# First feed-forward block of a two-layer kernel: seven block products of 384 columns in place of eight from the sixth feature on, and the residual kept in DRAM

## The chip, the cores and the metric

One Trainium2 chip; the kernel runs on one core. The metric is the device time of one launch in microseconds, the median of several runs. TensorE is called PE here, its weight loads PEld, VectorE DVE, ScalarE ACT, GpSimd POOL and SyncE SP. SP does nothing but issue transfers in this kernel; POOL may do so too.

## What is computed

A block with two layers on a sequence of 512 tokens and a context of 256 tokens, 1024 wide, all in 32-bit floats. Layer 0 mixes with Fourier transforms and a long convolution; layer 1 is attention over sequence and context. Each layer ends in a feed-forward block. Cut to that block, the reference is:

```python
def _conv_ffn(h, w_up, conv_w, conv_b, w_down):      # h: tokens x 1024, D_FF = 2816
    gate, val = jnp.split(h @ w_up, 2, axis=-1)
    return (jax.nn.silu(_dwconv3(gate, conv_w, conv_b)) * val) @ w_down

for i in range(2):
    sh1, sc1, g1, sh2, sc2, g2 = _adaln(c, w_mod[i], b_mod[i])   # silu(c) @ w_mod + b_mod
    ...
    x = x + g2 * _conv_ffn(_modulate(_rms_norm(x, norm2[i]), sh2, sc2), *ffn)
    if i == 0:
        ctx = ctx + cg2 * _conv_ffn(_modulate(_rms_norm(ctx, norm2[i]), csh2, csc2), *ffn)
```

In layer 0 the block therefore works on 768 columns (512 of x, 256 of the context); in layer 1 on 512. `w_up` has two halves, gate and value. The change is in the block of layer 0.

## The kernel before

**Layout.** Activations lie transposed: 128 features on the partitions, tokens along the free axis. 1024 features are 8 tiles (k = 0 to 7), 2816 are 22 tiles. A tile of 128 of the 2816 is called a feature f below, 0 to 21. The residual lives in SBUF in 8 tiles `xr` of 128 x 768.

**Products.** Each 32-bit operand is split into a high part in PE's reduced 32-bit format (`hi`, L247, on ACT) and the rest (`lo`, L252, on DVE: operand minus high part). `mm3` (L273 to L275) issues three matmuls for one product: high x high, high weight x low, low weight x high. So one 128 x 128 weight tile against n columns costs three matmuls of n columns, each with its own weight load.

**First feed-forward block** (`ffn` with `width == TV`, called by `layer0`). For each f, `products(f)` loads two weight tiles `w_up[0, f, 0]` (gate) and `w_up[0, f, 1]` (value) of 128 x 1024 by SP, splits them, and multiplies each by the 8 tiles of the normed activations, in two pieces of 512 (x, tiles `hh`, `hl`) and 256 columns (context, `hhc`, `hlc`): 2 x 8 x 2 x 3 = 96 matmuls. `up(f)` then does the convolution over three neighbouring tokens (`conv3`, L489 on ACT, L492 and L493 on DVE), silu (L1333), the product with the value half (L1335), and splits the result into `ah`, `al`. After 8, 16 and 22 features `res_proj` does the down-projection of that group: for each of the 8 output tiles m it loads and splits a tile of `w_dn`, multiplies it by the group's activations in the pieces 512 and 256, and adds the gated result to `xr[m]` straight out of PSUM (L1284, on DVE). The last group does all of x first and then all of the context, so that the norm of layer 1 starts beside the context's products; `ahook` also loads the first weights of attention.

**Work put in between.** The modulation vectors (`_adaln`) that are not needed yet are computed on DVE by `gemv_dve` (L358: a row product of a 128 x 1024 tile `wmodT` with the silu of the condition, one for x and one for the context where both are needed; L359 adds the bias). `fill(f)` does three of them after each f from 2 on. 56 tiles `wmodT` are left for this block; the first 24 have both conditions, the last 32 one.

**What sets the order.** In `ffn` of layer 0 the tile framework orders the instructions from the program's order. Other parts are written out by hand, token by token, in strings (`FILTER_ORDER`, `MIX_ORDER`, `ORDER`, `UP_ORDER`): inside `manual_schedule` each engine executes its instructions strictly in the written order. Every engine executes in order anyway: an instruction that waits holds up all that stands behind it on the same engine.

**Second feed-forward block** (`up1`, for layer 1). It is there already in the form that the change brings to layer 0, with blocks of 256 columns: from its fifth feature on the 2 x 2 blocks (gate and value, lower and upper four k, left and right half of the columns) are multiplied with seven block products instead of eight (Winograd's form of Strassen's scheme). Sums of weight blocks (`S1` to `S4`, L2170 to L2180) and, once, sums of activation blocks (`T1` to `T4`) are made on DVE; each has to be split again; the results are joined on ACT (`E1` to `E5`, L2228) and DVE (`C1`, `C2`, `V1`, `V2`, L2244 to L2257). Its order is `UP_ORDER`; its residual `xr` stays in SBUF and is added to by L2318 on DVE.

Of the kernel before, what the change touches and what calls it, by code (L numbers as in the profile page):

```python
# [28 lines left out]
GROUPS = ((0, 8), (8, 16), (16, 22))  # L29
# [117 lines left out]


# [12 lines left out]
class Ring:  # L161
# [9 lines left out]
    def put(self, t):  # L171
        self.left[id(t)] -= 1
        if not self.left[id(t)]:
            self.free.append(t)

# [15 lines left out]
class Builder:  # L191
# [159 lines left out]
    def gemv_dve(self, i, jt, conds=(0, 1), raw=None, row=None):  # L351

        nc = self.nc
        raw = raw or self.wraw(self.I["wmodT"][i, jt])
# [934 lines left out]
    def ffn(self, i, x, hh, hl, width, segs, first_segs, late, fill=None, hook=None, rest=None, early=False, there=()):  # L1289
        nc, I = self.nc, self.I  # L1290
        v = nc.vector
        if width == TV:
            self.gap("afit", 320)
            ax = self.pool("actx", bufs=10)
            self.gap("agap", 160)
            a1 = self.pool("act1")
            self.gap("agap2", 32)
            ac = self.pool("actc", bufs=9)
            act = lambda tag, f=1: Two(self.t(ax, [P, 512], F32R, tag), self.t(ac if f % 10 else a1, [P, 256], F32R, tag + "c"))
        else:  # L1300
            ap = self.pool("actx", bufs=10)
            act = lambda tag, f=1: self.t(ap, [P, T], F32R, tag)
        tm = self.pool(f"ftm{i}", bufs=3)
        acts = {}
        keep = []
        cuts = [slice(a, a + m) for a, m in segs]

        def products(f):
            ws = [self.wload(I["w_up"][i, f, q]) for q in range(2)]
            if early and f >= NF - 4:  # L1310

                n = 128 * (NF - GROUPS[2][0])
                keep.append((act("ah"), act("al")))
                raw = self.wraw(I["w_dn2"][i, len(keep) - 1], n)
                for c in cuts:
                    self.hi(keep[-1][0][:, c], raw[:, c])
                    self.lo(keep[-1][1][:, c], raw[:, c], keep[-1][0][:, c])
            pss = [self.mm(), self.mm()]
            if f == 0:
                todo = [(k, q, a, n) for seg in first_segs for k in range(KD) for q in range(2) for a, n in seg]  # L1320
            else:
                todo = [(k, q, a, n) for q in range(2) for a, n in segs for k in range(KD)]
            for k, q, a, n in todo:
                w = slice(128 * k, 128 * k + 128)
                self.mm3(pss[q][:, a : a + n], ws[q][0][:, w], ws[q][1][:, w], hh[k][:, a : a + n], hl[k][:, a : a + n], k == 0, k == KD - 1)
            return pss

        def up(f):
            pss = there[f] if f < len(there) else products(f)
            g = self.t(tm, [P, width], F32, "fg")  # L1330
            n = width
            self.conv3(g, pss[0], self.col(f"fcw{i}0", f), self.col(f"fcw{i}1", f), self.col(f"fcw{i}2", f), self.col(f"fcb{i}", f), segs)
            nc.scalar.activation(g[:, :n], g[:, :n], AF.Silu)  # L1333
            a = g
            v.tensor_tensor(a[:, :n], g[:, :n], pss[1][:, :n], op=ALU.mult)  # L1335
            ah, al = act("ah", f), act("al", f)
            for c in cuts:
                self.hi(ah[:, c], a[:, c])
                self.lo(al[:, c], a[:, c], ah[:, c])
            acts[f] = (ah, al)  # L1340
            if fill:
                fill(f)

        nxt = 0
        for gi, (f0, f1) in enumerate(GROUPS):
            while nxt < min(f1 + 1, NF):
                up(nxt)
                nxt += 1
# [1186 lines left out]
```

## Time and profile before

| | |
|---|---|
| median of 3 runs | 1526.65 us (1525.8 to 1541.0) |
| the profiled execution's own time | 1528.16 us |
| its span, first to last instruction | 1526.4 us |
| PE busy | 1500.2 us, 98% |
| PEld busy | 1305.4 us, 86% |
| DVE busy | 1153.6 us, 76% |
| ACT busy | 659.3 us, 43% |
| POOL busy | 93.6 us, 6% |
| granted PE clock, mean | 0.996 |
| moved from and to HBM | 169.1 MB, 111 GB/s over the span |

The profile is one execution. Rows of groups give a line of the kernel, engine, operation and tiles, the count, the busy time with the mean duration of one in ns, and the idle time of the engine just before them with what ended it. Durations of matmuls include their way through the array and overlap; the distance from one start to the next says what one costs. DVE's instructions overlap by a little less than 0.1 us in the same way. Rows of a window give, for each engine, busy us and the number of instructions in brackets.

### The profile page before, as it was taken

How to read it: one execution, taken by the hardware profiler on the slowest of the kernel's cores; microseconds unless marked ns; L12 is line 12 of the kernel's file. 1: busy time of each engine (PE TensorE's matmuls, PEld its weight loads, DVE VectorE, ACT ScalarE, POOL GpSimd, SP SyncE). 2: the span in 40 equal slices, each digit the busy share in tenths (PEclk: the TensorE clock that was granted, in tenths of full speed). 3: DMA queues.
4: the chain of work that ended last, by engine and by line, in shares of the span. 5: the costliest groups of instructions: out<-in, count | busy, mean ns of one | idle time of the engine just before them, and what ended most of it. 6: DMA issues, size and time to landing. Idle time of an engine off the chain costs nothing.

```text
span 1526.4 us, 24078 instructions
## 1 busy us (share of the span) xinstructions
PE 1500.2 (98%) x9728; PEld 1305.4 (86%) x9728; DVE 1153.6 (76%) x1979; ACT 659.3 (43%) x999; POOL 93.6 (6%) x110
## 2 busy tenths in 40 slices
PE   7999999999999999999999999999999999999999
PEld 5778888889888888888888897766559999999998
DVE  5799978888988346663355377999987899898873
ACT  4362235324323212222123235988964556555551
POOL 0021126000000000000000000111110000000000
PEclk9999999999999999999999999999999999999999
DMA  9426522452545234541344221000015223332322
GB/s 360 137 94 223 173 67 67 156 171 83 166 155 162 71 110 161 169 155 60 104 134 131 87 85 35 11 15 5 11 42 180 63 77 125 112 114 92 120 91 97
DMA packets 54987, 170.61 MB, mean 112 GB/s; under 512 B 6235, under 2 KB 9629, under 8 KB 53853
## 3 DMA queue, kind: packets, MB, share of 16 engines
q1 hardware_dynamic: 54877, 169.08, 33.2%
q8 instruction: 76, 1.25, 0.3%
q14 instruction: 34, 0.28, 0.1%
HBM read 163.29 MB, written 5.77 MB: 111 GB/s over the span
## 4 chain that ended last, share of the span: by engine, by line
PE 89%; DVE 5%; DMA 2%; ACT 1%; issue 1%; POOL 1%; SPq 0%; ACTq 0%; DVEq 0%; POOLq 0%
PE mm L273 16%; PE mm L274 16%; PE mm L275 16%; PE bank L273 7%; PE bank L275 7%; PE bank L274 7%; PE pv L1808 3%; PE s L273 2%; PE pv L1819 1%; PE s L275 1%; PE s L274 1%; PE ms L275 1%; PE ms L273 1%; PE ms L274 1%; DVE junk L358 1%
## 5 line engine op out<-in xcount | busy, mean ns | idle before, releaser
L247 ACT ACTIVATE wh<-wr 128x1024 fp32r<-128x1024 f32 (+2 forms) x170 | 168.4, 992 | 383.4 <-PE mm L274 272.5
L252 DVE TENSOR_TENSOR wl<-wr,wh 128x1024 fp32r<-128x1024 f32 (+2 forms) x170 | 194.9, 1148 | 51.1 <-ACT wh L247 48.7
L273 PE MATMUL mm<-hh,wh 128*128 128x512 f32 x504 | 198.8, 394 | 1.7 <-DVE tm L493 1.1
L274 PE MATMUL mm<-hl,wh 128*128 128x512 f32 x504 | 197.0, 391 | 2.3 <-DVE hl L428 2.3
L275 PE MATMUL mm<-hh,wl 128*128 128x512 f32 x504 | 196.6, 390 | 0.0
L358 DVE SCALAR_TENSOR_TENSOR junk<-wr,sb 128x1024 bf16<-128x1024 f32 x112 | 138.4, 1236 | 57.0 <-DMA wr<-wmodT 56.9
L274 PE MATMUL mm<-hlc,wh 128*128 128x256 f32 (+1 forms) x488 | 135.9, 279 | 0.0
L273 PE MATMUL mm<-hhc,wh 128*128 128x256 f32 (+1 forms) x488 | 135.9, 279 | 0.0
L275 PE MATMUL mm<-hhc,wl 128*128 128x256 f32 (+1 forms) x488 | 135.6, 278 | 0.0
L273 PEld LDWEIGHTS mm<-hh,wh 128*128 128x128 f32 x504 | 94.7, 188 | 22.4 <-issue 5.3
L275 PEld LDWEIGHTS mm<-hh,wl 128*128 128x128 f32 x504 | 94.6, 188 | 20.2
L274 PEld LDWEIGHTS mm<-hl,wh 128*128 128x128 f32 x504 | 94.7, 188 | 19.8 <-DVE hl L428 3.3
L1284 DVE SCALAR_TENSOR_TENSOR xr<-mm,mod,xr 128x512 f32<-128x512 f32 (+1 forms) x64 | 38.0, 615 | 86.1 <-PE mm L275 86.0
L275 PE MATMUL bank<-act,wl 128*128 128x256 f32 x352 | 97.3, 276 | 0.0
L273 PE MATMUL bank<-act,wh 128*128 128x256 f32 x352 | 97.2, 276 | 0.0
L274 PE MATMUL bank<-act,wh 128*128 128x256 f32 x352 | 97.2, 276 | 0.0
L273 PEld LDWEIGHTS mm<-hhc,wh 128*128 128x128 f32 x488 | 91.7, 188 | 3.9
L274 PEld LDWEIGHTS mm<-hlc,wh 128*128 128x128 f32 x488 | 91.6, 188 | 3.9
L275 PEld LDWEIGHTS mm<-hhc,wl 128*128 128x128 f32 x488 | 91.9, 188 | 0.0
L1760 ACT ACTIVATE S<-s,rks 128x512 f32<-128x512 f32 x96 | 63.1, 688 | 12.7 <-PE s L275 6.3
L275 PEld LDWEIGHTS bank<-act,wl 128*128 128x128 f32 x352 | 66.1, 188 | 0.1
L273 PEld LDWEIGHTS bank<-act,wh 128*128 128x128 f32 x352 | 66.1, 188 | 0.0
(604 smaller groups left out, 4136.8 us busy)
## 6 DMA issues: line engine op xcount, KB each, us to landing
wr<-w_up SPq DMA_DIRECT2D x88, 512.0 KB, 3.7
wr<-wmodT SPq DMA_DIRECT2D x80, 512.0 KB, 3.5
wr<-w_dx SPq DMA_DIRECT2D x24, 384.0 KB, 3.1
wm<-wmod0a SPq DMA_DIRECT2D x8, 1024.0 KB, 8.6
wr<-w_in SPq DMA_DIRECT2D x16, 512.0 KB, 4.3
wr<-w_dn SPq DMA_DIRECT2D x16, 512.0 KB, 3.5
wr<-w_out SPq DMA_DIRECT2D x11, 512.0 KB, 3.5
wr<-w_o SPq DMA_DIRECT2D x8, 512.0 KB, 3.5
```

Of the source, the lines that this page charges most:

```text
L247: self.nc.scalar.activation(dst, src, AF.Copy)
L252: (eng or self.nc.vector).tensor_tensor(dst, src, hi.bitcast(F32), op=ALU.subtract)
L273: mmul(out, wh, xh, start=start, stop=False, **kw)
L274: mmul(out, wh, xl, start=False, stop=False, **kw)
L275: mmul(out, wl, xh, start=False, stop=stop, **kw)
L358: nc.vector.scalar_tensor_tensor(junk, raw, 1.0, self.sb[:, j, :], op0=ALU.mult, op1=ALU.mult, accum_out=acc)
L1284: nc.vector.scalar_tensor_tensor(x[m][:, a2:b2], ps[:, a2 + o : b2 + o], mod[:, 8 * sec + m, c : c + 1], x[m][:, a2:b2], op0=ALU.mult, op1 ...
L1760: nc.scalar.activation(c.S[a, j // 3][:, j % 3, :], c.ps[a, j], AF.Copy, scale=c.s.r[:, g : g + 1])
L1808: nc.tensor.matmul(c.P[64 * a : 64 * a + 64, :], V[:, j, o : o + 64], c.S[a, j // 3][:, j % 3, :], start=j == 0, stop=j == 5, tile_positio ...
L1819: nc.tensor.matmul(c.zz[o : o + 32, :], self.ones32, c.S[a, h][:, i, :], start=i == 0, stop=i == 2, tile_position=(0, o))
```

## The change

- **Up-products of layer 0.** Features 0 to 4 stay plain, but the 768 columns are cut 384 + 384 instead of 512 + 256. From f = 5 on, seven block products `P1` to `P7` of 4 k-tiles x 384 columns take the place of eight. For them the weights get sums S1 to S4 (each 128 x 512) and three more splits (`HA`/`DA`, `H1`/`D1`, `H4`/`D4`, with `HG`/`DG`; plain features split gate and value only). The activations get sums T1 to T4 once (128 x 4 x 384 each, in halves), with T3 written over the right half of the lower k-tiles. The PSUM results are copied by ACT (`E1`, `E2`, `E3`, `E5`) and joined by DVE (`C1`, `C2`, `V1`, `V2`) in SBUF tiles `eg`, `ev`, from which the convolution and the product with the value half now read.
- **Groups of the down-projection.** Six groups (0-3, 4-6, 7-9, 10-12, 13-15, 16-21) for three; groups 0 to 4 in pieces of 384 + 384, the last in 256 + 256 and then 256.
- **Residual.** Before the block's sums begin, SP writes the 8 tiles `xr` to a DRAM tile `xq` each. Groups 0 to 4 don't add on DVE: ACT scales the PSUM result by the gate into one of two SBUF slots `st` (`XA`, three instructions), and POOL issues a transfer that adds the slot to `xq[m]` in DRAM (`XD`). Before the last group's adds SP loads `xq` back into new tiles `xr`; the last group adds on DVE as before.
- **Order.** The whole block from its first product on stands in a `manual_schedule` over PE, DVE, ACT, SP and POOL; its middle is a string `UP0_ORDER` of 1066 tokens, its beginning and end are written as code. 48 of the 56 tiles of `gemv_dve` are in the string (`LM` loads, `GV` computes), 8 in the end.
- **PSUM.** Six banks of 512 columns and two `ms` replace three tiles of two banks and two `ms`, for this block alone.

The core of the diff (the removed `ffn`, allocations, and parts that repeat the second block are cut):

```diff
-GROUPS = ((0, 8), (8, 16), (16, 22))
+GROUPS0 = ((0, 4), (4, 7), (7, 10), (10, 13), (13, 16), (16, 22))
+PLAIN0 = 5
+GEMV0 = 48
...
+UP0_ORDER = """
+LV:1 LG:2 LV:2 LM:0 LG:3 EA:0 GB:0 GV:0 LM:1 VB:0 HV:1 EB:0 DV:1 CV:0 LV:3 CX:0 GB:1 HG:2 GV:1 CC:0 LM:2 VA:1 DG:2 HV:2 SI:0 DV:2 LG:4 EA:1 EB:1 MU:0
...
+LW:1.1 DA:7 CV:6 GV:13 P7:6 XA:0.7 XD:0.7 HW:1.1 P1:7 CX:6 E3:6 LM:14 V2:6 CC:6 P2:7 V1:6 SI:6 S1:7 E1:7 MU:6 S3:7 AH:6 DW:1.0 H1:7 AL:6 DN:1.0 LW:1.2
...
+P7:21 HW:5.1 C2:21 CV:21 DW:5.1 CX:21 DN:5.0 HW:5.2 E3:21 DW:5.2 CC:21 V2:21 SI:21 DN:5.1 V1:21 MU:21 AH:21 AL:21 DN:5.2
+"""
...
+    def up0(self, x, H, hh, hl, steps, first, gl):
+        d0 = self.pool("d0", space=bass.MemoryType.DRAM)
+        xd = [self.t(d0, [P, TV], F32, f"xq{m}") for m in range(KD)]
...
+        W2 = TV // 2
+        cols = slice(0, W2), slice(W2, TV)
+        def piece(out, f, q, h, ks=range(KD)):
+            w = wt[f, q]
+            for k in ks:
+                s = slice(128 * k, 128 * k + 128)
+                self.mm3(out[:, 0:W2], w[0][:, s], w[1][:, s], hh[k][:, cols[h]], hl[k][:, cols[h]], k == 0, k == KD - 1)
+        def block(out, w, o, b, start):
+            for k in range(4):
+                s = slice(o + 128 * k, o + 128 * k + 128)
+                self.mm3(out[:, 0:W2], w[0][:, s], w[1][:, s], b[0][:, k, b[2]], b[1][:, k, b[2]], start and k == 0, k == 3, not start)
+        with self.tc.manual_schedule(engines={ENG.PE, ENG.DVE, ENG.Activation, ENG.SP, ENG.Pool}):
+            take, f2, a2 = steps
...
+            for k in range(KD):
+                for q in range(2):
+                    piece(ps[0, q, 0], 0, q, 0, [k])
+                if k == 0:
+                    take(KD)
+                if k == 2:
+                    f2(step=0)
+                if k == 6:
+                    f2(step=1)
+            ps[1, 0, 0] = R["mm"].get(1)
+            piece(ps[1, 0, 0], 1, 0, 0)
+            a2(0, 0)
...
+            for d in (5, 6, 7, 0, 1, 4, 2, 3):
+                nc.sync.dma_start(xd[d], x[d])
+            buffers()
...
+            def T(j, h):
...
+                if j in (1, 3):
+                    v.tensor_tensor(t_, part(plus, 0), part(less, 0), op=ALU.subtract)
+                    v.tensor_tensor(t_, t_, part(plus, 1), op=ALU.add)
+                    v.tensor_tensor(t_, t_, part(less, 1), op=ALU.subtract)
+                else:
+                    v.tensor_tensor(t_, part(plus, 0), u_, op=ALU.subtract)
+                    v.tensor_tensor(t_, t_, part(plus, 1), op=ALU.add)
+            def S1(f):
+                r = raw[f, 1]
+                v.tensor_tensor(r[:, half[1]], r[:, half[0]], r[:, half[1]], op=ALU.add)
+            def P1(f):
+                ps[f, "a"] = R["mm"].get(2)
+                block(ps[f, "a"], wt[f, 0], 0, up["B"][0], True)
+            def E1(f):
+                nc.scalar.copy(up["eg"][:, cols[0]], ps[f, "a"][:, 0:W2])
+            def join(dst, src):
+                v.tensor_tensor(dst, src[:, 0:W2], dst, op=ALU.add)
...
+            def XA(g, m):
+                p = ps.pop(("d", g, m))
+                s = st[g, m] = R["st"].get(1)
+                gate = lambda c: mod[:, 40 + m, c : c + 1]
+                nc.scalar.activation(s[:, 0:W2], p[0][:, 0:W2], AF.Identity, scale=gate(0))
+                nc.scalar.activation(s[:, W2:CX], p[1][:, 0 : CX - W2], AF.Identity, scale=gate(0))
+                nc.scalar.activation(s[:, CX:TV], p[1][:, CX - W2 : W2], AF.Identity, scale=gate(1))
+            def XD(g, m):
+                nc.gpsimd.dma_start(xd[m], st[g, m], accum_op=ALU.add)
+                R["st"].put(st.pop((g, m)))
+            def LM(i):
+                load(("m", i), I["wmodT"][gl[i][0], gl[i][1]], 1)
+            def GV(i):
+                self.gemv_dve(*gl[i], raw=raw["m", i])
...
+            LW(NL, 3)
+            get(0, 1)
+            LW(NL, 4)
+            get(2, 3)
+            split(3)
+            for m in range(KD):
+                if m < 3:
+                    DL(NL, m)
+                    for h in range(2):
+                        add(m, ps["d", NL, m][h], 256 * h, 256 * h + 256, 0)
+                else:
+                    p = R["mm"].get(1)
+                    for h in range(2):
+                        down(p[:, 256 * h : 256 * h + 256], NL, m, range(a, b), 256 * h, 256)
+                    add(m, p, 0, 512, 0)
+                if m:
+                    s1(m - 1)
+                if 1 <= m < 5:
+                    split(m + 3)
+                if m < 3:
+                    LW(NL, m + 5)
+                if m < 4:
+                    get(m + 4)
+                for i in left[m::KD]:
+                    LM(i)
+                    GV(i)
...
```

In the order string a token is a step and its argument: `P6:9` is the sixth block product of feature 9, `DN:1.4` the down-projection of group 1, output tile 4, `SG`/`SV` a plain gate or value product with both halves. `buffers()` makes, among others, the two slots `st`, six tiles `act` and two more raw weight tiles (five in all). `S2` to `S4` are built like `S1`, `P2` to `P7` like `P1`, one block each. In the code after the string `NL` is the last group, `get(m)` issues the load of `xr[m]` from `xq[m]` on SP, and `DL(NL, m)` multiplies only feature 21, since `DN:5.0` to `DN:5.2` have done the other five; after the part shown come the context's eight products with the norm of layer 1 between them.

More of the change, by code (lines that the diff above doesn't have):

```diff
@@ L174, in put, with get @@
             self.free.append(t)
+class Slots(Ring):
+    def get(self, uses):
+        make = self.free.pop(0)
+        t = make()
+        self.left[id(t)] = [uses, make, t]
+        return t
+    def put(self, t):
+        e = self.left[id(t)]
+        e[0] -= 1
+        if not e[0]:
+            self.free.append(e[1])
 class Cut:
@@ L353, in gemv_dve @@
         nc = self.nc
[L354 removed]
+        raw = self.wraw(self.I["wmodT"][i, jt]) if raw is None else raw
         for j in conds:
```

498 lines of the change are left out of this document (383 added, 115 removed).

## The prediction

> **What bounds the kernel now.** I read the page first: engine shares, then the chain that ended last.
>
> ```profile
> PE 1500.2 (98%) x9728; PEld 1305.4 (86%) x9728; DVE 1153.6 (76%) x1979; ACT 659.3 (43%) x999; POOL 93.6 (6%) x110
> ...
> GB/s 360 137 94 223 173 67 67 156 171 83 166 155 162 71 110 161 169 155 60 104 134 131 87 85 35 11 15 5 11 42 180 63 77 125 112 114 92 120 91 97
> ...
> PE 89%; DVE 5%; DMA 2%; ACT 1%; issue 1%; POOL 1%; SPq 0%; ACTq 0%; DVEq 0%; POOLq 0%
> ```
>
> PE holds 89% of the chain; the transfers (GB/s in 40 slices of 38 us) stay far below the 360 of the first slice nearly everywhere. Averages hide stages, so next come windows: one inside the first feed-forward block, the whole block (359 to 903 us), and the second block. The columns are window, length, then PE, PEld, DVE, ACT, POOL busy with counts, clock, DMA share, GB/s.
>
> ```profile
> 400.00:500.00 100.00, 100.00 (x590) 88.52 (x590) 83.77 (x162) 28.60 (x37) 0.00 (x0) 1.00 0.51 163
> ...
> 359.00:903.00 544.00, 543.84 (x3188) 480.66 (x3188) 325.35 (x581) 143.18 (x189) 0.00 (x0) 1.00 0.39 126
> 1200.00:1500.00 300.00, 299.97 (x2646) 299.72 (x2644) 264.69 (x391) 161.73 (x252) 0.00 (x0) 1.00 0.31 104
> ```
>
> In the block PE is busy 543.84 of 544 us at full clock while DVE works 325 and ACT 143. Nothing but PE's own work bounds it: fewer columns through PE are worth what they take, as long as the others keep up. The third row is the nearest evidence for that: the same seven-product scheme, with blocks of 256 columns, keeps PE at 299.97 of 300 us with DVE at 264.69 (88%).
>
> What one matmul costs is read from start to start in the timeline, here a run of 21 matmuls of 512 columns and then 24 of 256:
>
> ```profile
> 401.76 0.39 PE L273 MATMUL mm<-hh,wh 128*128 128x512 f32 x1
> ...
> 406.52 0.28 PE L273 MATMUL mm<-hhc,wh 128*128 128x256 f32 x1
> ...
> 409.26 0.39 PE L273 MATMUL mm<-hh,wh 128*128 128x512 f32 x1
> ```
>
> (406.52 - 401.76) / 21 = 226.7 ns for 512 columns, (409.26 - 406.52) / 24 = 114.2 ns for 256. The block has 22 x 96 = 2112 up-matmuls and 22 x 8 x 3 x 2 = 1056 down-matmuls, half of each width: 1584 x 0.2267 + 1584 x 0.1142 = 540.0 us of the 544. The rest is small norm matmuls and their restarts.
>
> **Part 1, PE.** After: up 5 x 96 + 17 x 84 = 1908 matmuls of 384 columns; down 16 features x 8 x 3 x 2 = 768 of 384; last group 6 x 8 x 3 x 3 = 432 of 256. So 204 matmuls of 384 columns go; the columns of the down-projection stay. The two prices above lie on a line through 0.44 ns a column, which gives 170.4 ns for 384. The trace has matmuls of 384 columns only in attention, where they are slower:
>
> ```profile
> 938.63 0.34 PE L275 MATMUL k<-wh,qal 128*128 128x384 f32 x1
> ...
> 940.19 0.34 PE L275 MATMUL k<-wh,qal 128*128 128x384 f32 x1
> ```
>
> 1.56 us for nine steps, 173.3 ns. I take 170.4, because those are short bursts and the block's are long and equal: 2676 x 0.1704 + 432 x 0.1142 = 505.3 us, **34.7 less**. At 173.3 it is 513.1, 26.9 less; that is one end of the range.
>
> **Part 2, DVE.** It gets weight sums, more splits, joins, activation sums; it loses the residual adds of the first 16 features. Its prices, start to start:
>
> ```profile
> 1299.18 0.42 DVE L2257 TENSOR_TENSOR vv<-ms,e 128x256 f32<-128x256 f32 x1
> 1299.51 0.68 DVE L252 TENSOR_TENSOR wl<-wr,wh 128x512 fp32r<-128x512 f32 x1
> ...
> 1301.97 0.68 DVE L252 TENSOR_TENSOR a2l<-wr,a2h 128x512 fp32r<-128x512 f32 x1
> 1302.57 1.22 DVE L252 TENSOR_TENSOR wl<-ss,wh 128x1024 fp32r<-128x1024 f32 x1
> 1303.71 0.75 DVE L2266 SCALAR_TENSOR_TENSOR fg<-gt,pcol,fg 128x511 f32<-128x511 f32 x1
> 1304.37 0.69 DVE L252 TENSOR_TENSOR act<-fg,act 128x512 fp32r<-128x512 f32 x1
> ```
>
> 0.33 us for 256 columns, 0.60 for 512, 1.14 for 1024, 0.66 for a convolution tap of 511. Between them: 0.47 for 384, 0.87 for 768, 0.39 for a tap of 255. One condition of the vector products:
>
> ```profile
> 399.62 1.23 DVE L358 SCALAR_TENSOR_TENSOR junk<-wr,sb 128x1024 bf16<-128x1024 f32 x1 [1.33 <-DMA wr<-wmodT]
> ...
> 400.97 1.22 DVE L358 SCALAR_TENSOR_TENSOR junk<-wr,sb 128x1024 bf16<-128x1024 f32 x1
> ```
>
> 1.35 us. Counted out of the written order, DVE has 58 instructions of 1024 columns, 70 of 768, 93 of 512, 110 of 384, 44 taps of each length and 72 conditions: 66 + 61 + 56 + 52 + 46 + 97 = 378 us, beside 453 us of PE in the same string (all of the block but its first 72 matmuls and its end). Over the whole that is 83%. It isn't even: from `SV:3` to `DN:0.4`, where the activation sums (20 instructions of 768) and their four splits fall, PE has 46.9 us and DVE 46.6; up to `P3:11`, while the vector products still have two conditions, PE 237 and DVE 212. In the dense stretch any wait of DVE reaches PE. I charge **+3 us** for that and for the new start; from below it is 0 (the second block's row above shows no loss), from above the rival below.
>
> ACT gets copies, `XA` and more splits: 204 thousand columns in the string. At L247's 992 ns for about a thousand
>
> ```profile
> L247 ACT ACTIVATE wh<-wr 128x1024 fp32r<-128x1024 f32 (+2 forms) x170 | 168.4, 992 | 383.4 <-PE mm L274 272.5
> ```
>
> that is some 200 us of 453: it hides beside PE, with 250 us to spare.
>
> **Part 3, the residual in DRAM.** No row shows an accumulating transfer. The nearest transfers:
>
> ```profile
> wr<-w_dx SPq DMA_DIRECT2D x24, 384.0 KB, 3.1
> ...
> xd<-xr SPq DMA_DIRECT2D x8, 256.0 KB, 2.0
> xr<-xd SPq DMA_DIRECT2D x8, 256.0 KB, 4.6
> ...
> sb<-cboth SPq DMA_DIRECT2D x2, 512.0 KB, 11.7
> ```
>
> First, eight writes of 384 KB now stand in SP's queue ahead of `LV:1` and all loads behind it. One after another at 1.5 x 2.0 us they take 24 us; at 200 to 360 GB/s 9 to 16. PE has six pieces of 24 matmuls, 24.5 us, whose weights are there before it needs `VA:1`, and the split of `LV:1` takes ACT and DVE 2 us: hidden unless they run singly, 3 us if they do.
>
> An accumulate reads and writes: 3.1 + 1.5 x 2.0 = 6.1 us at least, 1.5 x (4.6 + 2.0) = 9.9 by the slower read; 11.7 is the slowest row. I take 7, near the same size. What it may take follows from the order: `XA` of tile m + 2 needs the slot of m back. Between `XD:0.0` and `XA:0.2` PE has 6.1 us, between `XD:0.1` and `XA:0.3` 8.2, then 9.2 to 28.6, mostly 14 to 20. So at 7 us one slot is 1 us late, once, and PE has filled PSUM banks ahead: nothing. At 11.7 four slots are late by at most 5.6 + 3.5 + 2.5 + 1.5 = 13 us. Queued behind a waiting `XA` is all of ACT: weight splits, `E` copies, the convolution; PE follows within a block or two. POOL has nothing else to do; `XD` holds up nobody there.
>
> The Trainium skill, "DMA: Bandwidth & Descriptors", section "Anatomy of one DMA — SWDGE (gpsimd) path", gives 2.0 us plus bytes at 436 GB/s for a transfer issued by POOL; an estimate from it is 2.9 us, by which no slot is late; no run here shows one.
>
> At the end SP loads 8 x 384 KB of residual, five weight tiles and eight `wmodT`, 9 MB in one queue: a `get` that waits for an `XD` to land or for a tile to come free holds up the weights and `wmodT` behind it, and DVE's `GV` waits for those in order, with the adds and the norm's squares queued behind it. From the end of `P6:21`, which frees the first tiles, to the end of the x products PE has 37 us; at 360 GB/s the loads take 25, at 200 45. I charge nothing; 8 us is the other end.
>
> **The sum.** 1528.16 (profiled) - 34.7 + 3 = 1496.5. The median before lies 1.5 below its profiled execution, so the forecast is **1495**.
>
> **Rivals.**
>
> *DVE waits in order.* What speaks for it is how the vector products waited in the block before (groups by line, 359 to 903 us; the last number is idle time):
>
> ```profile
> L358 DVE SCALAR_TENSOR_TENSOR junk<-wr,sb 128x1024 bf16<-128x1024 f32 x80 | 97.8, 1222 | 55.5 <-DMA wr<-wmodT 55.5
> ```
>
> 55.5 us over 80 conditions, 0.69 each. Up to `P3:11` there are 51 conditions: 212 + 35 = 247 us against PE's 237, 10 us lost: 1505, and up to 1515 if the activation sums wait as well. Against it: those waits stood where DVE had time, and loads are now issued by a written order.
>
> *384 columns cost 173.3 ns.* 7.8 us more: 1503.
>
> *POOL holds up DVE.* The trace shows DVE beside POOL:
>
> ```profile
> 237.66 0.67 DVE L252 TENSOR_TENSOR s<-sx,s 128x512 fp32r<-128x512 f32 x1
> 237.82 1.66 POOL L1050 TENSOR_TENSOR sx<-sx,sx 128x512 f32<-128x512 f32 x1 [2.34 <-DVE sx L1045]
> ...
> 238.26 0.67 DVE L1042 TENSOR_TENSOR sx<-mm,s 128x512 f32<-128x512 f32 x1
> ```
>
> DVE's 512 columns take 0.67 us there as elsewhere, so I give it little. If each of the 20 `XD` up to `P3:11` held DVE for a POOL instruction of 1.66 us, 212 + 33 = 245 us against 237: 1503. The Trainium skill, "SBUF — State Buffer", section "Who interferes with whom", says that a DVE instruction with two SBUF inputs contends with POOL's reads; the row does not bear that out for DVE.
>
> *The two slots bound the block, and the kernel is slower.* Each slot goes round 19 times between its first and last `XA`, in 322 us of PE. With about 1.1 us of `XA` (768 columns at L247's price, in three) a transfer of 15.8 us begins to bind, 17.4 us (354 / 19 - 1.2) eats the gain, and each further us costs 19: at 18.5 us 1547. The slowest row is 11.7, which speaks against it.
>
> *The gain is not there*: the products go, but PE waits as long for seven split weight blocks as it saves. The time stays near 1525. Against it stands the second block's row.
>
> **How the numbers follow.** Forecast 0.56 (1488 to 1502); 384 columns slower 0.12; DVE's waits 0.15; POOL on DVE 0.03; slots late or the end late by some 10 us 0.06; no gain 0.03; slots bound 0.05. The range is 1487 (no loss, and 5 us of restarts gone) to 1513 (DVE's waits to their upper end nearly); about 1 in 10 lies above, less below. A measurement of this kernel tells about 1%, 15 us, from no change: faster than 1511 is 0.82 by these cases, within it 0.11, slower 0.07.
>
> **What would show it.** In the profile after: PE near 1465 us busy and still 98%; in the block some 2980 matmul records for 3188, the 384-wide ones 170 ns apart; DVE about 85% there without idle time put to `wmodT` of more than 10 us in the first 240 us; `XD` landing in 5 to 9 us, and no ACT wait for POOL's transfers; the attention stage as long as before. I am wrong if PE shows idle time in the block beyond 5 us: before `P6`/`P5` (activation sums late), before a `DN` (banks not freed, slots late), or at its end (norm late).

## The result, and the profile after

The changed kernel takes 1534.89 us (median of 20 runs, 1528.86 to 1545.07); the kernel before took 1526.18 beside it (20 runs, 1523.65 to 1541.0). The ratio is 1.0051, 95% interval 1.003 to 1.0071: it is slower, by less than the 1% named in the prediction, where 1495 was forecast and 1513 was the upper end of the range. The times of the kernel before fall into two groups, about 1523 to 1530 and 1533 to 1541, with 3 of the 20 runs here in the slower one and 54 of all 118 on record, so a ratio this near to 1 also moves with that share. The lowest of the changed kernel's 20 times is 5.2 us above the lowest of the kernel before. The profiled execution has a span of 1535.0 us, 8.6 more than before.

From the page of the changed kernel, busy times, the chain by engine, and the landing of the accumulating transfers:

```profile
PE 1490.2 (97%) x9668; PEld 1353.7 (88%) x9668; DVE 1268.5 (83%) x2150; ACT 774.0 (50%) x1236; POOL 128.1 (8%) x150
...
PE 85%; DVE 7%; DMA 2%; ACT 2%; issue 1%; POOL 1%; SPq 0%; ACTq 0%; DVEq 0%; POOLq 0%
...
xq<-st POOLq DMA_DIRECT2D x40, 384.0 KB, 5.6
```

PE is busy 10 us less and idle 19 us more. Windows of the changed kernel (columns as in the prediction): the start, the string before and behind a short wait near 517, and from the string's last products of 384 columns to attention's first product.

```profile
350.00:372.00 22.00, 18.81 (x122) 18.07 (x121) 13.90 (x32) 7.08 (x11) 0.00 (x0) 0.92 0.49 171
372.00:516.00 144.00, 144.00 (x817) 144.00 (x817) 128.35 (x216) 66.55 (x106) 7.19 (x8) 1.00 0.48 133
520.00:836.00 316.00, 316.00 (x1791) 316.00 (x1790) 254.75 (x421) 167.44 (x285) 27.61 (x32) 1.00 0.65 166
...
838.00:906.00 68.00, 58.70 (x449) 57.91 (x447) 42.85 (x89) 16.59 (x26) 0.00 (x0) 0.90 0.55 176
```

The string is as the prediction wanted it: apart from 0.5 us near 517 PE never waits, with DVE at 89% and 81%. Yet it is slower than forecast, because each product costs more. Two starts in the timeline of the changed kernel with 194 matmuls from the first to the last of them:

```profile
399.75 0.34 PE L337 MATMUL bank<-h0h,wl 128*128 128x384 f32 x1
...
433.85 0.34 PE L335 MATMUL bank<-h0h,wh 128*128 128x384 f32 x1
```

34.10 / 193 = 176.7 ns for 384 columns, not 170.4. At the end of the block PE waits. The chain of waits there, in order of time (start, duration, what), and the list of waits from 838 to 906 (total, times, longest):

```profile
852.97 5.16 DMA wr<-wmodT
858.16 1.25 DVE junk L420 x2
...
861.86 5.12 DMA wr<-wmodT
867.01 1.25 DVE junk L420 x2
868.27 4.05 DMA wr<-wmodT
...
875.95 5.87 DMA wr<-wmodT
```

```profile
DVE junk L420 <- DMA wr<-wmodT: 12.9, 4, 5.2
...
PE bank L337 <- DVE k6l L314: 2.8, 1, 2.8
PE ms L457 <- DVE nt L451: 2.7, 1, 2.7
...
PE bank L337 <- DVE k5l L314: 2.4, 1, 2.4
```

Four times DVE stands before a vector product (L420) whose 512 KB load was issued only right before it, and behind it in DVE's order stand the low part of the next weight tile of the last group (`k5l`, `k6l`) and the squares of the norm (`nt`), for which PE waits.

The starts of the same few products in the profile of every kernel below, read from the timelines, in us; "first score" is attention's first `s<-q,K`, and the last column is the spacing of 256-column products in most of the second feed-forward block, which none of the edits touches:

| kernel | out-projection ends | last 384 of the string | attention's first product | first score | span | spacing |
|---|---|---|---|---|---|---|
| before | 358.3 | | 903.6 | 966.1 | 1526.4 | 113.3 |
| after | 362.7 | 837.7 | 906.2 | 975.3 | 1535.0 | 113.3 |
| after, again | 360.3 | 835.3 | 901.3 | 972.0 | 1531.9 | 113.3 |
| e_gemv | 362.7 | 842.0 | 896.7 | 969.3 | 1539.6 | 117.8 |
| e_cuts | 363.4 | 831.9 | 899.4 | 970.1 | 1529.7 | 113.3 |
| e_start | 359.6 | 833.9 | 900.5 | 972.5 | 1543.5 | 117.8 |
| e_end | 361.9 | 837.6 | 892.3 | 964.9 | 1535.4 | 117.8 |
| e_early | 361.6 | 834.3 | 900.5 | 975.2 | 1545.4 | 117.8 |
| e_best | 362.3 | 832.0 | 885.9 | 959.9 | 1519.6 | 113.3 |
| e_nudge | 361.0 | 832.4 | 898.0 | 970.6 | 1530.2 | 113.3 |
| e_comb | 366.5 | 835.8 | 889.9 | 959.0 | 1529.7 | 117.8 |
| e_best2 | 362.5 | 832.0 | 884.2 | 959.7 | 1530.1 | 117.8 |
| e_bank | 361.8 | 831.1 | 885.2 | 954.3 | 1525.7 | 117.8 |

From the first score to the end the kernels of this table with 113.3 ns need 559.6 to 560.3 us and those with 117.8 need 570.2 to 571.4. Two profiled spans can therefore be compared only at one spacing; the first score stands for the part that the edits reach.

Before against after, the 8.6 us are: block -1.7 (out-projection's end to attention's first product, 545.2 to 543.5), out-projection later by 4.3, attention's first product to first score 6.6 longer (62.5 to 69.1), the rest -0.6.

### The profile page after: what moved, and what is told of

Same layout as the page of the kernel before. It is cut to its first block, busy times and chain, and to the rows that moved or that the text cites. A ratio compares the mean times of both kernels' runs of the same rounds, so it can differ in the third digit from the quotient of the medians.

```text
span 1535.0 us, 24574 instructions
## 1 busy us (share of the span) xinstructions
PE 1490.2 (97%) x9668; PEld 1353.7 (88%) x9668; DVE 1268.5 (83%) x2150; ACT 774.0 (50%) x1236; POOL 128.1 (8%) x150
## 4 chain that ended last, share of the span: by engine, by line
PE 85%; DVE 7%; DMA 2%; ACT 2%; issue 1%; POOL 1%; SPq 0%; ACTq 0%; DVEq 0%; POOLq 0%
PE bank L335 16%; PE bank L337 16%; PE bank L336 16%; PE mm L335 4%; PE mm L337 4%; PE mm L336 4%; PE pv L2257 3%; PE ms L337 3%; PE ms L336 3%; PE ms L335 3%; DMA wr<-wmodT 2%; PE s L335 2%; DVE junk L420 2%; PE pv L2268 1%; PE s L336 1%; PE s L337 1%
## 5 line engine op out<-in xcount | busy, mean ns | idle before, releaser
L420 DVE SCALAR_TENSOR_TENSOR junk<-wr,sb 128x1024 bf16<-128x1024 f32 x83 | 102.5, 1235 | 18.9 <-DMA wr<-wmodT 18.9
L337 PE MATMUL bank<-act,bl 128*128 128x384 f32 x256 | 86.6, 338 | 0.5 <-DVE bl L314 0.5
L336 PE MATMUL bank<-act,bh 128*128 128x384 f32 x256 | 86.5, 338 | 0.0
L335 PE MATMUL bank<-act,bh 128*128 128x384 f32 x256 | 86.5, 338 | 0.0
L336 PEld LDWEIGHTS bank<-act,wh 128*128 128x128 f32 x406 | 77.1, 190 | 0.0
L335 PEld LDWEIGHTS bank<-act,wh 128*128 128x128 f32 x406 | 77.1, 190 | 0.0
L335 PE MATMUL bank<-h0h,wh 128*128 128x384 f32 x216 | 73.3, 339 | 0.0
L336 PE MATMUL bank<-h0l,wh 128*128 128x384 f32 x216 | 73.0, 338 | 0.0
L337 PE MATMUL bank<-h0h,wl 128*128 128x384 f32 x216 | 73.0, 338 | 0.0
L335 PE MATMUL mm<-hh,wh 128*128 128x512 f32 x152 | 62.5, 411 | 6.2 <-ACT wh L309 3.0
L336 PE MATMUL mm<-hl,wh 128*128 128x512 f32 x152 | 60.4, 397 | 2.3 <-DVE hl L490 2.3
L337 PE MATMUL mm<-hh,wl 128*128 128x512 f32 x152 | 60.4, 398 | 0.0
L2231 DVE TENSOR_TENSOR S<-S,mx 128x1536 f32<-128x1536 f32 x32 | 54.8, 1743 | 1.1 <-POOL mx L2227 1.1
L309 ACT ACTIVATE wh<-ss 128x1024 fp32r<-128x1024 f32 x36 | 38.2, 1061 | 33.9 <-PE bank L336 27.2
```

The source lines that it names most:

```text
L309: self.nc.scalar.activation(dst, src, AF.Copy)
L335: mmul(out, wh, xh, start=start, stop=False, **kw)
L336: mmul(out, wh, xl, start=False, stop=False, **kw)
L337: mmul(out, wl, xh, start=False, stop=stop, **kw)
L420: nc.vector.scalar_tensor_tensor(junk, raw, 1.0, self.sb[:, j, :], op0=ALU.mult, op1=ALU.mult, accum_out=acc)
L2231: v.tensor_tensor(c.S[a, h], c.S[a, h], mb.to_broadcast([P, 3, T]), op=ALU.subtract)
```

## The experiments

**What a product costs.** `e_widths` puts matmuls alone into the changed kernel:

```diff
+w, x_ = acts[16], acts[17]
+for n, c in ((512, 0), (448, 0), (416, 0), (384, 0), (384, 384), (352, 0), (320, 0), (256, 0), (192, 0), (128, 0), (384, 0), (512, 0)):
+    p = R["mm"].get(1)
+    for i in range(20):
+        o = 128 * (i % 6)
+        self.mm3(p[:, 0:n], w[:, o : o + 128], w[:, TV + o : TV + o + 128], x_[:, c : c + n], x_[:, TV + c : TV + c + n], i == 0, i == 19)
+    R["mm"].put(p)
```

> Added ahead of the last down-products, as PE work whose results nobody uses: 60 matmuls each at 512, 448, 416, 384, 384 (the second half of the columns), 352, 320, 256, 192, 128, 384 and 512 columns, same 128 x 128 weights and operands, in the same order of high and low parts as everywhere, while the other engines run dry. Theory 'width': a matmul of 384 columns costs 175.4 ns by its width alone, so the three series of 384 lie at 175 to 176 ns here too, with 512 at 226.7 and 256 at 114. Rival 'traffic': the 175.4 of the string comes from the transfers and VectorE work beside it, so 384 lies at 170 to 171 ns here. Either way the span grows by about 112 us.

A window in the middle of the series (DVE, ACT, POOL and DMA at zero), and the first start of each series in its timeline:

```profile
845.00:888.00 43.00, 43.00 (x235) 42.09 (x234) 0.00 (x0) 0.00 (x0) 0.00 (x0) 1.00 0.00 1
```

```profile
831.25 0.40 PE L334 MATMUL bank<-act,act 128*128 128x512 f32 x1
...
844.87 0.36 PE L334 MATMUL bank<-act,act 128*128 128x448 f32 x1
...
857.03 0.35 PE L334 MATMUL bank<-act,act 128*128 128x416 f32 x1
...
868.23 0.33 PE L334 MATMUL bank<-act,act 128*128 128x384 f32 x1
...
889.06 0.32 PE L334 MATMUL bank<-act,act 128*128 128x352 f32 x1
...
907.51 0.28 PE L334 MATMUL bank<-act,act 128*128 128x256 f32 x1
...
914.71 0.25 PE L334 MATMUL bank<-act,act 128*128 128x192 f32 x1
...
921.39 0.24 PE L334 MATMUL bank<-act,act 128*128 128x128 f32 x1
...
928.06 0.39 PE L334 MATMUL bank<-act,act 128*128 128x384 f32 x1
```

Differences over 60 (120 for the first 384): 227.0 ns for 512, 202.7 for 448, 186.7 for 416, 173.6 for 384 (173.3 once it runs), 120.0 for 256, 111.3 for 192, 111.2 for 128. Neither theory holds as written: in quiet 384 costs 173.3, between the 175.4 of the one and the 170 to 171 of the other, and not the 176.7 of the string. In this series 256, 384 and 512 columns lie on one line, of (227.0 - 120.0) / 256 = 0.42 ns a column. The line that the prediction drew began at the 114.2 that 256 columns cost in the block before, 6 ns below this one, so its point for 384 came out too low. At 192 and 128 columns the width no longer matters. The Trainium skill, "TensorE: Matmul & The Clock Gate", section "LDWEIGHTS (loading the stationary operand)", gives P / 1.2 ns for a load of P columns of weights; for 128 columns that is an estimate of 106.7 ns, 4.5 short of the floor of 111.2 measured here. The section "Back-to-back issue gap" there gives N / 2.4 + 2.5 ns for an isolated matmul of N columns; for 384 that is an estimate of 162.5 ns, and every spacing of 384 measured here is at least 10.8 above it.

**Why 176.7 in the string.** Several of these kernels run the same instructions up to 500 us or more. In the timeline of `e_early`, 196 matmuls from the first to the last of these two:

```profile
399.68 0.34 PE L337 MATMUL bank<-h1h,wl 128*128 128x384 f32 x1
...
433.48 0.34 PE L337 MATMUL bank<-h1h,wl 128*128 128x384 f32 x1
```

33.80 / 195 = 173.3, where the changed kernel had 176.7 with the same program, tiles and transfers. Read the same way over the whole string, the timelines show three levels. The changed kernel and `e_gemv` ran at 176.7 from 372 on, `e_end` too until 815 and then at 173.3. `e_early` had 173.3 until 471, 174.7 until its short wait at 514 and 176.7 from there; `e_widths` had 173.3 until 471 and 174.7 from then on; `e_start` had 176.7 until its short wait at 518, 173.3 until 590 and 174.7 from there. The repeat of the changed kernel:

> The changed kernel once more, unchanged. Theory 'phase': the spacing of 384 columns in the string is drawn anew by each execution's start (362 to 372) and at the short wait near 517, so this profile may show 173.3, 174.7 or 176.7 there, and the stalls of the end at the same instructions as before whatever the spacing; its runs spread over 1528 to 1545. Rival 'the spacing belongs to the program': 176.7 from 372 to 836 again.

It was 176.7 again, before and behind the short wait, with the stalls of the end at the same instructions; alone it would have spoken for the rival. `e_nudge` breaks the train of equal products:

```diff
 def P1(f):
     block(ps[f, "a"], wt[f, 0], 0, up["B"][0], True)
+    nc.tensor.matmul(ps[f, "a"][:, 384:448], wt[f, 0][0][:, 0:128], up["B"][0][0][:, 0, 0:64], start=True, stop=True)
```

> The change, with one added product of 64 columns (its result unused) in each feature from the sixth on, 17 in all and under 2 us. Theory 'the spacing is a phase that holds until PE's train of equal products is broken': the spacing of products of 384 columns changes level at some of the 17 places between 173.3, 174.7 and 176.7 ns. Rival 'the level is set by what the products read or by the traffic': it stays where it was, 176.7 throughout if the start is as in the change's own run.

(The added product opens an accumulation in a bank where another is still open and so changes that sum; the instructions are otherwise the same.) The spacing was 176.7 until the first added product at 462. From there it was 173.3, then 174.7, 176.7, 174.7, 176.7, 174.7, and 173.3 from 629 to the end of the string: seven changes, each from one of the 17 added products on. The string ended 5.3 us earlier than the changed kernel's (832.4 to 837.7; 1.7 of it was there at the out-projection) although 17 products were added. So the spacing is one of a few levels, each held for a hundred equal products or more, and a short interruption can change it. It is not needed for a change: at 471 in `e_early` and `e_widths` and at 590 in `e_start` the level moved inside a train in which PE did not wait. Traffic, tiles and the program do not set the level on their own, since the same instructions ran at all three; what in PE makes the levels the runs do not show.

**Cutting at 512 + 256 again**, where the products are plain:

```diff
-self.mm3(out[:, 0:W2], ..., hh[k][:, cols[h]], hl[k][:, cols[h]], k == 0, k == KD - 1)
+self.mm3(out[:, 0 : PN[h]], ..., hh[k][:, PC[h]], hl[k][:, PC[h]], k == 0, k == KD - 1)   # PC = 0:512, 512:768
...
-down(p[h][:, 0:W2], g, m, range(a, b), W2 * h, W2)
+down(p[h][:, 0 : PN[h]], g, m, range(a, b), CX * h, PN[h])
```

> The plain up-products of the first five features and the down-products of the first five groups are cut at 512 + 256 columns in place of 384 + 384; block products stay at 384. Theory 'width': 624 pairs go from 350.8 ns to 226.7 + 114.2 = 340.9 ns, 6.2 us less, 1528.5. Rival 'traffic': 512 and 256 columns pay the same share beside the transfers (about 233 + 117), no gain, within 1.5 us of 1535.

The time did not move measurably (ratio to before 1.0009, 0.9981 to 1.0038, for 1.003 to 1.0071 of the change). In the profile the string ends 5.8 us earlier, near the 6.2 expected, but for another reason: in the first features the pair cost 233.2 + 117.8 = 351.0 ns, nearly the 353.4 of two 384s, while the block products ran at 173.3 instead of 176.7 (1428 x 3.4 = 4.9 us). All five kernels with this cut show 173.3 for most of the string; with it, widths alternate between the blocks.

**The end of the block.** `e_gemv` takes the eight vector products out of it:

```diff
-GEMV0 = 48
+GEMV0 = 56
 # order string, features 19 to 21: LM:48 to LM:55 and GV:48 to GV:55 put in, LW:5.0 to LW:5.2 put later
```

> The eight matrix-vector products that stood between the last down-products (with their 512 KB loads) are put into the string over features 19 to 21; the three loads of weights of the last group that were issued early there go later, to free their buffers. Nothing else changes. Theory 'VectorE waits in order': the 28 us that the chain after the change gives to these loads go, PE keeps its clock, attention's first product moves from 910 to 888-892, and the time falls by 18 to 24 us to 1511-1517. Rival 'the end is bound by its other loads' (residual, kept weights): the same stalls show at other instructions and the time falls by less than 6 us.

From the string's last 384 to attention's first product 54.7 us instead of 68.5, so the stalls were these loads: 13.8 us in the changed kernel's profile. (The five other profiles with this end, `e_after`, `e_cuts`, `e_start`, `e_early` and `e_nudge`, have 65.6 to 67.5 us there, so 11 to 13 us.) But the forecast for the total failed. DVE had no room where I put the products, and PE waited in the string instead:

```profile
819.68 0.44 PE L336 MATMUL bank<-T2h,wl 128*128 128x384 f32 x1 [2.33 <-DVE wl L313]
```

The string ended 4.3 us later, and of the 13.8 us 6.0 were left at the first score; the ratio to before is 1.0022 (0.9982 to 1.0061). `e_end` puts two of them into the string and leaves six in the end with their loads ahead:

```diff
-for i in left[m::KD]:
-    LM(i)
-    GV(i)
+for i in {3: (0,), 5: (1, 2), 6: (3,), 7: (4, 5)}.get(m, ()):
+    GV(left[i])
+for i in {0: (0,), 3: (1, 2), 4: (3,), 5: (4, 5)}.get(m, ()):
+    LM(left[i])
```

> Of the eight matrix-vector products at the end, two go into the string (features 19 and 20), six stay between the last down-products, but each load is issued about 8 us ahead of its product, once a buffer is free, in place of right before it. Theory 'VectorE waits in order for a load issued too late': PE runs without a stall from 838 on, attention's first product lies 53 to 55 us behind the string's last product of 384 columns (68 us after the change, 55 us with all eight in the string) and the string does not stall at 817 as it did with all eight. About 14 us less in the block, some 9 of them left at the end of the run, since attention's start then waits for its norm. Rival 'the end cannot hold these products and their 512 KB each beside the residual and the kept weights': over 60 us.

Again 54.7 us, with six of the eight loads still in the queue; the window of `e_end` from 838 to attention's first product:

```profile
838.00:892.00 54.00, 51.29 (x448) 50.70 (x446) 40.16 (x82) 16.45 (x26) 0.00 (x0) 1.00 0.64 206
```

PE does in 54 us what took it 68 (448 products to 449), at full clock, and the transfers move 206 GB/s for 176. The loads fitted; they were issued too late. The string kept a stall of 0.6 us at 817, where the expectation had none. The first score came 10.4 us earlier (964.9; some 9 expected); the ratio is 0.9993 (0.9959 to 1.0027).

**The start.** In the changed kernel PE waits for the last weight of the out-projection, whose splits stand behind those of the first up-weights, and then runs at half rate (0.21 us for 260 columns, 0.12 at full clock):

```profile
358.73 0.58 PE L337 MATMUL mm<-yh,wl 128*128 128x260 f32 x1 [2.12 <-DVE wl L314]
...
361.07 0.42 PE L335 MATMUL mm<-yhc,wh 128*128 128x260 f32 x1
361.28 0.42 PE L336 MATMUL mm<-ylc,wh 128*128 128x260 f32 x1
```

```diff
-for f, q in ((0, 0), (0, 1)) if stage and j == 6 else ((1, 0),) if stage and j == 7 else ():
+for f, q in ((0, 0), (0, 1), (1, 0)) if stage and j == 7 else ():
```

> The loads and splits of the first three up-weights come after the last out-projection weight instead of ahead of it. Theory 'a moved split': the 3.2 us of idle PE at 355-359 and the half clock for 2.7 us behind it (1.3 us lost) go, and the time falls by 3 to 4.5 us. Rival 'the norm bounds the start': PE waits as long, at the first up-product in place of the last out-projection, and the time is within 1 us.

The out-projection ended 3.1 us earlier, but the wait only moved to the first up-products:

```profile
362.64 0.44 PE L337 MATMUL bank<-h0h,wl 128*128 128x384 f32 x1 [1.11 <-DVE wl L314]
```

The first down-product started at 449.5, in the changed kernel at 449.2. The rival was right in effect; the time did not fall (ratio 1.0044, 1.0018 to 1.0071).

**The handover to attention.** The windows right behind attention's first product, before and after:

```profile
903.00:923.00 20.00, 20.00 (x107) 17.11 (x106) 16.02 (x42) 8.95 (x19) 0.00 (x0) 1.00 0.16 55
```

```profile
905.00:925.00 20.00, 15.79 (x64) 12.20 (x65) 14.42 (x33) 6.90 (x12) 0.00 (x0) 0.83 0.28 86
```

PE stands 4 of 20 us and runs part of the rest at half rate: 64 products for 107. The longest stand there is this wait:

```profile
910.11 0.80 PE L335 MATMUL mm<-hh,wh 128*128 128x512 f32 x1 [2.95 <-ACT wh L309]
```

`e_early` moves work on DVE forward:

```diff
+if j in (1, 2, 3):
+    aw[name] = self.wload(src)          # was at j in (4, 5, 6)
-if j >= 3:
-    for d in ((0, 1, 2), (3,), (4, 5), (6,), (7,))[j - 3]:
+if j >= 2:
+    for d in ((0,), (1, 2), (3,), (4, 5), (6,), (7,))[j - 2]:
...
-    take(KD - 1)
+    take(2 * j - 7)
```

> The change as it is, but in the context part of the last down-products attention's first three weights are loaded and split two steps earlier and the norm is applied one step earlier, the squares of the context spread over the steps. Theory 'VectorE's order at the handover': the 3.4 us wait for a weight's high part behind attention's first product and the half clock after it go; the 69.1 us from attention's first product to its first score product fall to 62-64 us (62.5 before the change), 5 to 7 us of the total. Rival 'the norm itself bounds the handover': first product later by as much as the rest is shorter, under 2 us.

My theory fell. The first wait went, but another came a few us later, for the context's squares,

```profile
909.88 0.58 PE L457 MATMUL ms<-ones,nt 128*128 128x1 f32 x4 [2.43 <-DVE nt L451]
```

and the first score stood at 975.2, as without the edit (975.3), though the string had been 3.4 us shorter. A second wait, of the same 2.38 us, is in every profile after the change; in the kernel before the same product starts without one:

```profile
949.19 0.45 PE L335 MATMUL k<-wh,qah 128*128 128x384 f32 x1 [2.38 <-DVE kp L2053]
```

Its bank was the suspect (`e_bank`, on the combination below):

```diff
+for _ in range(1):
+    self.mm()
 pqa = self.mm()
```

> The cuts and the end with six products in it, and one change more: attention's three accumulators start one pair of banks later, so that the first product of queries takes the banks of the accumulator that is read out first, not of the one that VectorE still reads. Theory 'the 2.65 us wait that every changed kernel shows ahead of this product, and the kernel before does not, comes from the bank it is given': the wait goes with its half clock, and the first score product moves from 959.0 to 954-957, profiled 1515-1517 with the second feed-forward at 113.3 ns (1526-1528 at 117.8), 10 us under the kernel before at the same spacing. Rival 'VectorE brings its operands that late anyway': the wait stays, within 1 us of 959.

The wait stayed, 2.38 us again, and so did the 69.1 us from the first product to the first score. Its first score of 954.3 is 4.7 us earlier than `e_comb`'s because its out-projection ended 4.7 us earlier, ahead of every edit. Moving the fold of the squares behind more products did not help either (`e_best2`, which is `e_comb`, `e_early` and this edit):

```diff
-qa(5, (0,)); f2(tp, 0); ...; qa(5, (1,)); qa(6); qa(7); f2(tp, 1)
+qa(5); qa(6); f2(tp, 0); ...; qa(7); kx(0); kx(1); kx(2); f2(tp, 1)
```

> As the last, with attention's weights and norm early, and attention's fold of the context's squares moved behind the seventh step of its first product and the spread behind three steps of the next, so that PE has work while VectorE sums. Theory 'PE waits in order for sums that VectorE brings late': the stalls of 1.4 us at the end's norm and 2.9 us behind attention's fifth step go with their half clock; first score product at 952 to 955, profiled 1512-1515 at 113.3 ns, 11 to 14 us under the kernel before. Rival 'VectorE is the bound of the whole handover': first score product at 959 or later as without it.

959.7, the rival's figure. What the traces do settle is where the time lies. Three starts on DVE split it, first in the kernel before, then in the changed one: the last add of the context's residual (`xr`), the first step of the context's norm behind its sum (`nrm_s`), and `kp`.

```profile
907.95 0.49 DVE L1284 SCALAR_TENSOR_TENSOR xr<-mm,mod,xr 128x256 f32<-128x256 f32 x1
...
910.95 0.16 DVE L400 TENSOR_SCALAR nrm_s<-ms 128x2 f32<-128x2 f32 x1 [1.52 <-PE ms L395]
...
939.76 1.00 DVE L1604 SCALAR_TENSOR_TENSOR kp<-mm,pcol,ropeK 64x768 f32<-64x768 f32 x1
```

```profile
915.55 0.48 DVE L1821 SCALAR_TENSOR_TENSOR xr<-bank,mod,xr 128x256 f32<-128x256 f32 x1
...
919.33 0.16 DVE L462 TENSOR_SCALAR nrm_s<-ms 128x2 f32<-128x2 f32 x1 [0.76 <-PE ms L457]
...
948.13 1.00 DVE L2053 SCALAR_TENSOR_TENSOR kp<-mm,pcol,ropeK 64x768 f32<-64x768 f32 x1
```

From attention's first product to the norm it is 7.4 us before and 13.1 after, from the norm to `kp` 28.8 both times, from `kp` to the first score 26.4 and 27.2. So 5.7 us lie ahead of the norm, where DVE makes its last add of the context 9.3 us behind attention's first product instead of 4.4, and 0.8 us behind `kp`, with the second wait (0.8 to 3.8 in the other changed kernels of the table without `e_early`'s edit). `e_early` brought the norm to 10.0 us behind the first product, but then `kp` came 32.0 us later and the first score another 32.7. The 6.6 us are thus located, mostly in DVE's work ahead of the context's norm, but not explained: two edits of the order and one of the banks did not shorten the way to the first score. The order of DVE's and ACT's work there was the tile framework's before and is written by hand since the change; which of its dependences holds was not settled.

**The parts together.** `e_best` is `e_end`, `e_early` and `e_cuts` in one; `e_comb` is `e_cuts` and `e_end` alone, with the last vector product moved behind the norm's last square.

> The two edits above together with the cuts at 512 + 256 columns. Sum of the parts: string 5.8 us shorter, end 14 us shorter, handover 5 to 7 us shorter: first score product at 975 - 26 = about 949 (966.1 before the change), profiled 1508 with the second feed-forward at 113.3 ns a product of 256 columns, 1520 with it at 117.8. Rival 'one wait takes the place of another': attention's own chain after its first product holds the first score product at 960 or later.

> The cuts at 512 + 256 columns and the end with two products in the string and six with their loads ahead (now none between the last full product and the norm's sum), attention's handover left as the change has it. Theory 'the parts add': string 5.8 us, end 14 us, so first score product at about 958, 1518 with the second feed-forward at 113.3 ns (1508 if nothing were given back at the handover), some 5 us under the kernel before at the same spacing. Rival 'DVE-bound handover': first score product no earlier than 964.9, as with the end alone.

| kernel | median (runs) | before beside it | ratio, 95% interval |
|---|---|---|---|
| after, again | 1541.23 (12) | 1526.95 | 1.0058 (1.0022 to 1.0094) |
| e_early | 1533.73 (10) | 1528.19 | 1.0021 (0.9989 to 1.0052) |
| e_best | 1526.36 (12) | 1528.19 | 0.9974 (0.9944 to 1.0004) |
| e_comb | 1523.01 (12) | 1526.95 | 0.9962 (0.9929 to 0.9995) |
| e_best2 | 1525.35 (12) | 1526.95 | 0.9967 (0.9933 to 1.0001) |
| e_bank | 1524.52 (12) | 1535.66 | 0.9948 (0.9915 to 0.9982) |

The sum of the parts did not come out in `e_best`: its first score of 959.9, for 949 forecast, is the rival's. `e_comb`'s 959.0 is near the 958 forecast, though its out-projection had ended 3.9 us later than the changed kernel's.

`e_comb` and `e_bank` come out ahead of both kernels, by little, and `e_bank`'s ratio flatters it: the kernel before had a median of 1535.66 beside it, 9 us above the 1526.95 beside `e_comb`; against that, its median would be 0.998. The string and the end gave what the single edits had shown (e_comb: 469.3 us from the out-projection's end to the string's last 384, for 475.0 after the change; 54.1 us of end for 68.5), and by the difference in the handover 6.6 us more would be there, which no run shows.

## Why the prediction was wrong, point by point

- **The step that failed first is a term of the sum**: 384 columns at 170.4 ns, a straight line between 512 and 256, with 173.3 as the other end. Measured: 173.3 in quiet and 176.7 in the profiled string. 2676 x 6.3 ns = 16.9 us, less 0.4 for 256 columns at 113.3: +16.5. The lower end of the straight line, 114.2 for 256, does not lie on the line of 0.42 ns a column that 256 to 512 columns show in one series (120.0 to 227.0). The row of attention that I set aside as short bursts had the price in quiet, and even this end of the range was too low.
- **The second is the end of the block**, charged at nothing with 8 us as the other end. It cost 13.8 in the profiled execution (68.5 to 54.7). I had compared the queue's bytes with PE's time, which was right (`e_end`), and named DVE's in-order wait for `wmodT`, but not priced it as a chain: the load is issued when a buffer is free, lands in 4 to 6 us, and only then does DVE go on to what PE needs.
- The small norm products and restarts went from 5.2 to about 8 us (475.1 - 472.9 in the string, 54.7 - 48.9 in the end without stalls); that is the +3 of the sum. Block: forecast -31.7, measured -1.7; 16.5 + 13.8 closes it to 0.3.
- **Outside the block** the prediction had "the attention stage as long as before" and only the +3 for the new start. The out-projection ended 4.3 us later (`e_start`: some 3 of it is the moved split, but nothing is gained by moving it back; in the other changed kernels it ended at 360.3 to 366.5, so part of it differs from one execution to the next). The handover was 6.6 longer, mostly ahead of the context's norm on DVE.
- **DVE waits in order**: the right mechanism in the wrong place. In the string, where I priced it, DVE waits only 3.9 us for `wmodT`, in four waits, and none of it reaches PE, not even in the dense stretch at 89%.
- **Right**: the accumulating transfers (7 us taken, 5.6 measured, no slot late), ACT hidden, no sign of POOL on DVE (the split of 1024 columns takes 1.22 us beside an `XD` and without), PE saturated through the string. The slower side came out, but not by the rival that stood for it: two slots bind from 15.8 us a transfer. The estimate of 2.9 us from the Trainium skill, "DMA: Bandwidth & Descriptors", section "Anatomy of one DMA — SWDGE (gpsimd) path", was too low for these transfers.
- One sign was miscounted: "204 matmuls go" leaves out that the last group, cut in three, has 432 where it had 288. Only 60 go, 3198 to 3138 records from the out-projection's end to attention's first product, and not 3188 to 2980. The sum has the right counts.
- The rule "wrong if PE shows idle time at its end" pointed to the right place.

## What to carry to other kernels

Price a matmul by a row of its own width in a long train, and take the worst level such a train shows, not a line between two other widths that may run at different levels. A load that is issued right before its use costs its landing time on the engine that waits, and everything behind it in that engine's order, however much bandwidth is left; issue it a few steps ahead. When one block is rewritten, the microseconds before and behind it, where the engines hand over, have to be priced too: here they cost 11 us.

## What the hardware showed that I had not expected

Equal products run at one of a few spacings: 384 columns at 173.3, 174.7 or 176.7 ns, 256 at 113.3 or 117.8 (120.0 in one series), with the clock at 1.00 throughout. In the second feed-forward block, whose instructions are the same in all these kernels, two profiles show it, `after` and `e_gemv`:

```profile
1400.00:1450.00 50.00, 50.00 (x444) 50.00 (x443) 43.35 (x64) 26.63 (x42) 0.00 (x0) 1.00 0.29 99
```

```profile
1400.00:1450.00 50.00, 50.00 (x427) 50.00 (x426) 42.44 (x63) 25.60 (x40) 0.00 (x0) 1.00 0.28 96
```

444 products for 427, and 10.6 us from the first score to the end. Whether these levels also make the spread of the times is not shown: each profile is one execution.

PE's clock halves after shorter breaks than I had thought. In `e_best` PE waits once for DVE and then runs a row of tiny norm products:

```profile
870.16 1.05 PE L456 MATMUL ms<-ones,nt 128*128 128x1 f32 x8 [1.11 <-DVE nt L450]
```

```profile
871.00:876.00 5.00, 5.00 (x31) 5.00 (x32) 4.37 (x15) 1.06 (x1) 0.00 (x0) 0.66 0.34 99
```

1.11 us of idle time and the 0.9 us of tiny products behind it were enough for a granted clock of 0.66 over the next 5 us. The Trainium skill, "TensorE: Matmul & The Clock Gate", section "HAM oscillation — how this bites in real kernels", puts the limit at idle gaps of about 3.4 us; this row shows a third of that, with nearly idle products beside it.
